# Row kurtosis on one core: more row sums on VectorE from whole-row loads, and wide dummy matmuls in the tail

## Chip, core and metric

The kernel runs on one NeuronCore of a Trainium2 chip. The metric is the device time of one execution in microseconds, given as the median over several runs. Less is better.

## What is computed

The input `x` has 1024 rows of 8192 float32 values. For each row the kernel returns the excess kurtosis:

```python
mean = np.mean(x, axis=-1, keepdims=True)
std = np.std(x, axis=-1, keepdims=True)
z = (x - mean) / (std + 1e-8)
return (np.mean(z ** 4, axis=-1) - 3).astype(np.float32)
```

So every element is read once from HBM (33.55 MB) and is used three times: in the row's sum (for the mean), in the sum of squared deviations, and in the sum of their fourth powers.

## The kernel before

**Groups.** The rows are cut into 18 groups, numbered 0 to 17 (`GROUPS`, L16). An entry is (k, pieces, elements of ACT, engine of the sum). A row is spread over k partitions, so a group has 128/k rows and a tile of 128 x 8192/k. From group 3 on k is 2 and a tile is 128 x 4096 float32, 2.1 MB. `pieces` says into how many DMAs the tile's load is cut and how wide each is. The last entry says which engine adds up the row: 'DVE' (VectorE), 'PE' (TensorE), or 'both' for the last group.

**Loads.** `load(i)` issues the DMAs of group i on SyncE's queue (L134). There are five tile buffers (`SLOT_OF`, L39). `load_next` issues a load only after the group that held the buffer before is through its fourth powers, and in program order.

**Mean (`mean`, L163).** In a 'DVE' group `added_halves` (L157) runs one VectorE instruction, which adds the left half of the tile to the right half and accumulates over the row; it needs the whole tile. A small matmul with a block matrix (L167) then adds up the k partitions of a row. In a 'PE' group `transposed_sums` (L140) runs 32 transposes of 128 x 128 which accumulate into one PSUM tile `tps`; they can start with the first piece. VectorE reduces that tile (`pair_sums`, `red`, L146), and a small matmul (L176) gives the mean. In both cases ScalarE copies the result to `nmu` (L178). In what follows "the mean matmul" is L167 or L176.

**Squares and fourth powers.** `square` (L184) is one ScalarE instruction over the tile, which writes (x - mean)^2 in place and accumulates it. `fourth_act` (L191) squares the first columns again on ScalarE, as many as the group's entry says; `fourth_dve` (L196) does the other columns on VectorE.

**Order.** The order is written out by hand. Iteration i of the main loop (L266) issues: `mean(i)`, `square(i)`, `fourth_dve(i-1)`, the next load, steps of `finish`, `fourth_act(i)`. Each engine runs its own instructions in that order. So VectorE reduces or adds up group i before it does the fourth powers of group i-1, and TensorE starts the transposes of group i+1 behind the mean matmul of group i.

**Finish.** `finish` (L210) turns the sums of a batch of groups into results, in three steps: matmul `p` (L225), reciprocal and `fac` on VectorE; then `sq` on ScalarE, matmul `pf`, `frow` on ScalarE; then matmuls `pk` (L243), `kr` on VectorE and the output DMA (L247). `STEPS` (L260) says in which iterations the three steps of the first three batches are issued.

**Tail.** The last group's squares are done in two halves, and its fourth powers are split between both engines. `keep_busy(n)` (L205) issues n dummy transposes of a tile of zeros, whose result nobody reads: 28 after the first matmul of the last `finish`, 12 after its third (L217 to L223).

Of the kernel before, what the change touches and what calls it, by code (L numbers as in the profile page):

```python
# [7 lines left out]
f32 = mybir.dt.float32  # L8
# [3 lines left out]
P = 128  # L12
# [5 lines left out]
    (8, [1024], 0, 'DVE'),  # L18
    (4, [2048], 0, 'DVE'),
    (2, [4096], 1280, 'DVE'),  # L20
    (2, [4096], 768, 'DVE'),
    (2, [4096], 1536, 'DVE'),
    (2, [2304, 1792], 640, 'PE'),
    (2, [2304, 1792], 640, 'PE'),
    (2, [2304, 1792], 640, 'PE'),
    (2, [2304, 1792], 640, 'PE'),
    (2, [2304, 1792], 512, 'PE'),
    (2, [2304, 1792], 512, 'PE'),
    (2, [2304, 1792], 512, 'PE'),
    (2, [2304, 1792], 512, 'PE'),  # L30
    (2, [1536, 1536, 1024], 512, 'PE'),
    (2, [1536, 1536, 1024], 512, 'PE'),
    (2, [1536, 1536, 1024], 512, 'PE'),
# [9 lines left out]
def kernel(  # L43
# [5 lines left out]
    nc = tc.nc  # L49
# [14 lines left out]
    psfin = ctx.enter_context(tc.tile_pool(name="psfin", bufs=1, space=bass.MemoryType.PSUM))  # L64
    ctx.enter_context(tc.manual_schedule())

    zeros = const.tile([P, 512], f32, name="zeros")
# [21 lines left out]
    ident = const.tile([P, P], f32, name="ident")  # L89
# [108 lines left out]
            op0=AO.mult, op1=AO.add, accum_out=quads[1 + second][:, j:j + 1])  # L198


    idle = psfin.tile([P, P], f32, name="idle")

    def keep_busy(n):
        for _ in range(n):
            nc.tensor.matmul(idle, lhsT=zeros[:, :P], rhs=ident, start=True, stop=True,  # L205
                             is_transpose=True)

    def finish(b):  # L210
        s2, quads = stats[b[0]]
        n = len(b)
        k = KS[b[0]]
        r = P // k
        sel = blk[k].rearrange("p (r k) -> p r k", k=k)[:, :, 0]
        p2 = psfin.tile([P, n], f32, name="p2")
        if b[-1] == L:  # L217
            nc.tensor.matmul(p2[:, :n - 1], lhsT=blk[k], rhs=s2[:, :n - 1], start=True, stop=True)
            keep_busy(28)
            for j in (0, 1):  # L220
                nc.tensor.matmul(p2[:, n - 1:], lhsT=blk[k], rhs=s2[:, n - 1 + j:n + j],  # L221
                                 start=j == 0, stop=j == 1)
            keep_busy(12)  # L223
        else:
            nc.tensor.matmul(p2, lhsT=blk[k], rhs=s2, start=True, stop=True)  # L225
        rec = fin.tile([P, n], f32, name="rec")
        nc.vector.reciprocal(rec, p2)
        fac = fin.tile([P, n], f32, name="fac")
        nc.vector.scalar_tensor_tensor(
            out=fac, in0=rec, scalar=-1.0, in1=rec, op0=AO.mult, op1=AO.mult)  # L230
        yield
        sq = fin.tile([P, n], f32, name="sq")
        nc.scalar.activation(out=sq, in_=p2, func=AF.Square)
        pf = psfin.tile([n, r], f32, name="pf")
        nc.tensor.matmul(pf, lhsT=fac, rhs=sel, start=True, stop=True)  # L235
        frow = fin.tile([n, r], f32, name="frow")
        nc.scalar.activation(out=frow, in_=pf, func=AF.Copy, scale=-float(n_cols) / k)
        yield
        pk = psfin.tile([n, r], f32, name="pk")
        terms = [(q, sel) for q in (quads[1], quads[0])] + [(sq, sel3[k])]  # L240
        terms += [(q, sel) for q in quads[2:]]
        for j, (t, m) in enumerate(terms):
            nc.tensor.matmul(pk, lhsT=t, rhs=m, start=j == 0, stop=j == len(terms) - 1)  # L243
        kr = fin.tile([n, r], f32, name="kr")
        nc.vector.tensor_mul(kr, pk, frow)
        dst = out[ROWS[b[0]]:ROWS[b[-1] + 1]].rearrange("(g r) -> g r", r=r)
        nc.sync.dma_start(out=dst, in_=kr)  # L247
# [5 lines left out]
    def load_next(done):  # L253
        while to_load and held.get(SLOT_OF[to_load[0]], -1) <= done:
            i = to_load.pop(0)
            held[SLOT_OF[i]] = i
            load(i)

    load_next(-1)
    STEPS = [(7, 8, 9), (9, 10, 11), (13, 14, 15)]  # L260
    steps = {}
    for b, ats in zip(BATCHES[:-1], STEPS):
        f = finish(b)
        for at in ats:
            steps.setdefault(at, []).append(f)
# [11 lines left out]
    a = GROUPS[L][2]  # L277
    h = n_cols // KS[L] // 2
    f = finish(BATCHES[-1])
    mean(L)  # L280
    square(L, h, 2 * h)
# [38 lines left out]
```

## Time and profile before

| what | value |
|---|---|
| median of 7 runs | 98.27 us (97.74 to 98.72) |
| the profiled execution: its own time | 97.97 us |
| the profiled execution: span of the core's instructions | 96.3 us |
| PE, DVE, ACT busy | 61.5, 75.7, 79.9 us |
| busy share of the main DMA queue | 84.8% of the span |
| HBM read | 33.55 MB |
| last load lands | 84.7 us after the span's start |

PE is TensorE, DVE is VectorE, ACT is ScalarE, SP is SyncE. Times within the profile are counted from the span's start. Busy shares are means over an opening, a long steady part and a tail. Between the end of the span and the execution's own time lie 1.7 us that no instruction shows.

### The profile page before, as it was taken

What the parts mean: (1) busy time and instruction counts of PE and PEld (TensorE: products, weight loads), DVE (VectorE), ACT (ScalarE), POOL (GpSimd) and SP (SyncE); (2) the same over time, 40 slices, a digit from 0 to 9 for tenths busy, and PEclk for the clock granted to TensorE, in tenths of its full rate; (3) what the DMA queues carried; (4) which work ended last, traced back from release to release, by engine and by line L of the source; (5) the groups of instructions that cost most, each with busy time, mean ns of one, the idle gap of its engine ahead of it and who ended that gap; (6) DMA issues with size and microseconds to landing.
All of it is one profiled execution on the core that took longest, in us unless ns stands there. A gap on an engine that the chain in (4) does not pass through costs nothing.

```text
span 96.3 us, 1389 instructions
## 1 busy us (share of the span) xinstructions
PE 61.5 (64%) x504; PEld 57.2 (59%) x504; DVE 75.7 (79%) x77; ACT 79.9 (83%) x96; POOL 6.1 (6%) x22
## 2 busy tenths in 40 slices
PE   0040201011099797979797979797979797969670
PEld 0040201010099696969696969696969696959560
DVE  2256719899994394989797979699999797999960
ACT  6065350999999699999999999999999998999950
POOL 6980000000000000000000000000000000000000
PEclk9999999999999999999999999999999999999999
DMA  2999999999999999999999999999999999400000
GB/s 89 371 344 429 429 429 436 436 429 409 406 435 365 430 417 439 421 414 422 426 417 425 419 406 430 415 411 408 421 412 416 409 419 401 188 0 7 0 0 4
DMA packets 5083, 33.65 MB, mean 350 GB/s; under 512 B 596, under 2 KB 596, under 8 KB 3540
## 3 DMA queue, kind: packets, MB, share of 16 engines
q1 hardware_dynamic: 5076, 33.56, 84.8%
q8 instruction: 4, 0.07, 0.3%
q14 instruction: 3, 0.02, 0.1%
HBM read 33.55 MB, written 0.00 MB: 349 GB/s over the span
## 4 chain that ended last, share of the span: by engine, by line
PE 42%; ACT 25%; DMA 14%; DVE 13%; issue 3%; DVEq 0%
PE tps L140 32%; ACT xt L184 21%; DMA xt<-in_x_dram 14%; DVE junk L157 5%; DVE xt L196 4%; DVE red L146 4%; PE mps L176 3%; ACT xt L191 2%; PE pk L243 2%; PE idle L205 1%; PE mps L167 1%; ACT nmu L178 1%; PE pf L235 1%; PE p L225 1%; PE p L221 0%
## 5 line engine op out<-in xcount | busy, mean ns | idle before, releaser
L184 ACT ACTIVATE xt<-xt,nmu 128x4096 f32<-128x4096 f32 (+2 forms) x19 | 60.4, 3178 | 0.6
L196 DVE CUSTOM_DVE_ANT_0 xt<-xt 128x3584 f32<-128x3584 f32 (+7 forms) x19 | 59.4, 3130 | 0.9 <-ACT xt L184 0.6
L140 PE MATMUL tps<-ident,xt 128*128 128x128 f32 x380 | 46.5, 282 | 0.0
L140 PEld LDWEIGHTS tps<-ident,xt 128*128 128x128 f32 x380 | 43.9, 147 | 0.9 <-DMA xt<-in_x_dram 0.4
L167 PE MATMUL mps<-part,blk 128*128 128x1 f32 x12 | 3.4, 350 | 23.8 <-DVE part L157 23.8
L167 PEld LDWEIGHTS mps<-part,blk 128*128 128x128 f32 x12 | 3.0, 311 | 24.1 <-ACT xt L184 9.2
L157 DVE CUSTOM_DVE_ANT_0 junk<-xt 128x2048 bf16<-128x2048 f32 (+3 forms) x7 | 10.1, 1448 | 7.1 <-DMA xt<-in_x_dram 7.1
L191 ACT ACTIVATE xt<-xt 128x512 f32<-128x512 f32 (+5 forms) x15 | 12.5, 832 | 0.4
L178 ACT COPY nmu<-mps 128x1 f32<-128x1 f32 x18 | 2.8, 155 | 11.2 <-PE mps L167 9.5
L146 DVE TENSOR_REDUCE red<-tps 128x128 f32<-128x256 f32 x12 | 5.1, 424 | 8.3 <-PE tps L140 8.3
L176 PEld LDWEIGHTS mps<-negcol,red 128*128 128x128 f32 x22 | 3.3, 188 | 8.7 <-DVE red L146 3.0
L176 PE MATMUL mps<-negcol,red 128*128 128x1 f32 x22 | 4.0, 251 | 6.3 <-DVE red L146 4.5
L205 PE MATMUL idle<-ident,zeros 128*128 128x128 f32 x40 | 4.8, 274 | 0.0
L205 PEld LDWEIGHTS idle<-ident,zeros 128*128 128x128 f32 x40 | 4.5, 145 | 0.0
L184 ACT ACTIVATION_READ_ACCUMULATOR xt<-xt,nmu 128x1 f32 x19 | 3.5, 186 | 0.0
L191 ACT ACTIVATION_READ_ACCUMULATOR xt<-xt 128x1 f32 x15 | 2.8, 186 | 0.0
L79 POOL TENSOR_SCALAR_AFFINE_SELECT blk<-blk 128x128 f32<-128x128 f32 x3 | 2.1, 716 | 0.2
L69 ACT ACT_TABLE_LOAD x1 | 1.3, 1283 | 0.8 <-PEq L304 0.8
L243 PE MATMUL pk<-blk,q 128*5 128x64 f32 (+3 forms) x18 | 1.7, 217 | 0.0
L82 POOL TENSOR_SCALAR_AFFINE_SELECT blk<-blk 128x128 f32<-128x128 f32 x3 | 1.6, 542 | 0.2
L196 DVE DVE_READ_ACCUMULATOR2_ANT q<- 128x1 f32 x19 | 1.6, 82 | 0.0
L68 DVE MEMSET zeros<- 128x512 f32 x1 | 0.5, 485 | 1.0 <-PEq L304 1.0
(33 smaller groups left out, 16.4 us busy)
## 6 DMA issues: line engine op xcount, KB each, us to landing
xt<-in_x_dram SPq DMA_DIRECT2D x8, 1152.0 KB, 11.0
xt<-in_x_dram SPq DMA_DIRECT2D x8, 896.0 KB, 12.5
xt<-in_x_dram SPq DMA_DIRECT2D x3, 2048.0 KB, 11.1
xt<-in_x_dram SPq DMA_DIRECT2D x7, 768.0 KB, 11.2
xt<-in_x_dram SPq DMA_DIRECT2D x5, 512.0 KB, 11.3
xt<-in_x_dram SPq DMA_DIRECT2D x1, 1024.0 KB, 7.2
xt<-in_x_dram SPq DMA_DIRECT2D x1, 640.0 KB, 11.6
xt<-in_x_dram SPq DMA_DIRECT2D x1, 384.0 KB, 10.6
```

The source lines that it names most:

```text
L79: nc.gpsimd.affine_select(out=v, in_=v, pattern=[[-k, r], [0, k]], base=0, channel_multiplier=1, compare_op=AO.is_ge, fill=0.0)
L140: nc.tensor.matmul(tps, lhsT=xts[i][:, c:c + P], rhs=ident, start=c == 0, stop=c == w - P, is_transpose=True)
L146: nc.vector.tensor_reduce(out=red.rearrange("p (r k) -> p r k", k=2), in_=tps.rearrange("p (r k) -> p r k", k=2).unsqueeze(2).to_broadcast ...
L157: nc.vector.tensor_tensor_reduce(out=junk[:, :h], in0=t[:, :h], in1=t[:, h:], scale=1.0, scalar=0.0, op0=AO.add, op1=AO.add, accum_out=part)
L167: nc.tensor.matmul(mps, lhsT=blk[k], rhs=added_halves(i, 0), start=True, stop=True)
L176: nc.tensor.matmul(mps, lhsT=pair_sums(tps), rhs=negcol, start=True, stop=True)
L178: nc.scalar.copy(nmu, mps)
L184: nc.scalar.activation(out=t, in_=t, func=AF.Square, bias=nmus[i], accum_out=s2[:, j + second:j + second + 1])
L191: nc.scalar.activation(out=t, in_=t, func=AF.Square, accum_out=quads[0][:, j:j + 1])
L196: nc.vector.tensor_tensor_reduce(out=t, in0=t, in1=t, scale=1.0, scalar=0.0, op0=AO.mult, op1=AO.add, accum_out=quads[1 + second][:, j:j + 1])
L205: nc.tensor.matmul(idle, lhsT=zeros[:, :P], rhs=ident, start=True, stop=True, is_transpose=True)
L243: nc.tensor.matmul(pk, lhsT=t, rhs=m, start=j == 0, stop=j == len(terms) - 1)
```

## The change

Groups 6 and 7 become 'DVE' groups: their tiles are loaded by one DMA each instead of two, and VectorE adds up the rows; groups 8 to 13 stay 'PE' with two pieces. The number of columns whose fourth powers ACT does changes in groups 4 to 13. The finish steps of the first two batches are issued two iterations later. In the tail 28 and 12 dummy transposes of 128 columns become 4 and 1 dummy matmuls of 512 columns, of zeros by zeros.

```diff
     (2, [4096], 1280, 'DVE'),
-    (2, [4096], 768, 'DVE'),
+    (2, [4096], 1024, 'DVE'),
+    (2, [4096], 1152, 'DVE'),
+    (2, [4096], 1280, 'DVE'),
     (2, [4096], 1536, 'DVE'),
-    (2, [2304, 1792], 640, 'PE'),
-    (2, [2304, 1792], 640, 'PE'),
-    (2, [2304, 1792], 640, 'PE'),
-    (2, [2304, 1792], 640, 'PE'),
-    (2, [2304, 1792], 512, 'PE'),
-    (2, [2304, 1792], 512, 'PE'),
-    (2, [2304, 1792], 512, 'PE'),
-    (2, [2304, 1792], 512, 'PE'),
+    (2, [2304, 1792], 576, 'PE'),
+    (2, [2304, 1792], 576, 'PE'),
+    (2, [2304, 1792], 576, 'PE'),
+    (2, [2304, 1792], 576, 'PE'),
+    (2, [2304, 1792], 576, 'PE'),
+    (2, [2304, 1792], 576, 'PE'),
     (2, [1536, 1536, 1024], 512, 'PE'),
...
-    idle = psfin.tile([P, P], f32, name="idle")
+    idle = psfin.tile([P, 512], f32, name="idle")
 
     def keep_busy(n):
         for _ in range(n):
-            nc.tensor.matmul(idle, lhsT=zeros[:, :P], rhs=ident, start=True, stop=True,
-                             is_transpose=True)
+            nc.tensor.matmul(idle, lhsT=zeros[:, :P], rhs=zeros, start=True, stop=True)
...
-            keep_busy(28)
+            keep_busy(4)
...
-            keep_busy(12)
+            keep_busy(1)
...
-    STEPS = [(7, 8, 9), (9, 10, 11), (13, 14, 15)]
+    STEPS = [(9, 10, 11), (11, 12, 13), (13, 14, 15)]
```

## The prediction

> **What bounds the kernel now.** I read the busy slices first. From slice 1 on the DMA row is full until 84 us, and PE starts its long work only in slice 11:
>
> ```profile
> PE   0040201011099797979797979797979797969670
> ...
> DMA  2999999999999999999999999999999999400000
> ```
>
> A full DMA row does not say that anybody waits for it. The view of waits does:
>
> ```profile
> DVE red L146 <- PE tps L140: 8.3, 11, 2.9
> ...
> PEld tps L140 <- DMA xt<-in_x_dram: 0.4, 2, 0.2
> ```
>
> Once the PE groups run, the transposes wait 0.4 us in all for loads, while VectorE's reduction waits for the transposes in 11 groups. So the steady part goes at the pace of a loop through PE and DVE: 32 transposes, reduction, mean matmul, and only then the next 32. PE's timeline shows it, and its start:
>
> ```profile
> 26.60 0.56 PE L167 MATMUL mps<-part,blk 128*128 128x1 f32 x2 [4.67 <-DVE part L157]
> 27.02 5.86 PE L140 MATMUL tps<-ident,xt 128*128 128x128 f32 x32
> 33.48 0.35 PE L176 MATMUL mps<-negcol,red 128*128 128x1 f32 x2 [0.61 <-DVE red L146]
> 33.70 3.69 PE L140 MATMUL tps<-ident,xt 128*128 128x128 f32 x32
> 38.00 0.35 PE L176 MATMUL mps<-negcol,red 128*128 128x1 f32 x2 [0.61 <-ACT xt L184]
> 38.21 0.36 PE L225 MATMUL p<-s,blk 128*128 128x2 f32 x2
> 38.44 3.69 PE L140 MATMUL tps<-ident,xt 128*128 128x128 f32 x32
> 42.73 0.35 PE L176 MATMUL mps<-negcol,red 128*128 128x1 f32 x2 [0.61 <-ACT xt L184]
> ```
>
> A bare lap, from one mean matmul to the next, is 38.00 - 33.48 = 4.52 us. With a finish step in it it is 4.65 to 4.99. The mean matmul of group 16 comes at 81.41, so groups 8 to 16 take 81.41 - 42.73 = 38.68 us. A group's bytes need 5.0 us (the trace's records of the loads' semaphores have the last pieces of groups 10 and 16 at 49.67 and 79.67: 30.0 us for six groups). So the loop gains on the loads by about 0.2 us a lap, and just catches up: in group 13 and in group 17 a piece is late by 0.1 us each. ACT is third in line: it runs back to back, idle before `nmu` for 1.08 us at 33.87 and hardly again. Three queues thus end within half a microsecond of each other, and whatever falls behind by more sets the end.
>
> The first lap matters most. Group 6's 32 transposes take 5.86 us, the next group's 3.69. No load explains it, since group 6 is complete at 28.62. The window view of L140 counts the transposes:
>
> ```profile
> 27.10:31.30 4.20, 4.20 (x20) 4.20 (x21) 1.00 0.98 388
> 34.00:37.20 3.20, 3.20 (x32) 3.15 (x29) 1.00 1.00 420
> ```
>
> 20 in 4.2 us against 32 in 3.2 us (each count has some that overlap an edge); start to start it is 213 ns until 31.5 and 109 ns after. The array starts from rest at half speed and needs 4.5 us of work to rise. (The column after the counts, the granted clock, says 1.00 for both; this trace's record of it begins only with the rise at 31.48, so the spacing is what to read.) The price is 5.86 - 3.69 = 2.17 us, paid once.
>
> **The change, part by part.** *Where PE starts.* Groups 6 and 7 go to DVE, so the start from rest moves to group 8. DVE's order is then: halves of 5, fourths of 4, halves of 6, fourths of 5, halves of 7. Up to 26.37 nothing changes. From start to start a halves-add takes 2.21 us (18.93 to 21.14), the fourths of 2816 columns 3.02 (21.14 to 24.16) and of 3328 columns 3.54 (26.37 to 29.91), so by the straight line 3072 columns take 3.28 and 2944 take 3.15. Fourths of 4 start at 26.37, halves of 6 at 29.65 (the tile landed at 28.62), fourths of 5 at 31.86, halves of 7 at 35.01 (landed 33.93). Before, group 5's halves started at 24.16 and the first transposes at 27.02, 2.86 us later. So group 8's transposes start at 35.01 + 2.86 = 37.87, against 38.44 now: 0.57 us earlier, and group 8's first piece landed at 36.73.
>
> *The start from rest.* Now from first transpose to mean matmul it is 33.48 - 27.02 = 6.46 us cold, 42.73 - 38.44 = 4.29 warm. Group 8's mean matmul comes at 37.87 + 6.46 = 44.33 instead of 42.73: **+1.60 us**. Bounds: 0 extra if PE were already at full speed (as at 33.70), and 32 x (213 - 109) ns = 3.3 if the whole group ran slow. I take 2.17, the one row that shows a start after such sparse work: in both kernels PE has before it only a pair of mean matmuls every 5 us.
>
> The Trainium skill speaks against the move here: TensorE: Matmul & The Clock Gate, Part 1, says that the array idles at half clock, rises after about 3.4 us of sustained work, and that its window runs freely, so the ramp differs from run to run. By its 3.4 us, an estimate, 16 transposes would be slow, 1.7 us instead of 2.17, and the sum below would be 0.5 smaller. Part 4 of the same page says that transposes do not raise the clock; the trace disagrees, for nothing but transposes ran from 27.02 to the rise at 31.48.
>
> *The loop behind it.* Groups 8 to 16 have the same laps. The first `p` step (0.21 us: 42.73 - 38.00 less 4.52) now lies inside this stretch; the lap of group 13 loses its late piece (66.96 - 62.23 = 4.73 without a step, 0.21 over a bare one). They cancel: 38.68 us again. The loop cannot win the 1.60 back, because its own latency is its pace; that the loads land 5.0 us apart no longer matters when it runs behind them.
>
> *ACT.* Fourths on ACT grow from 9728 to 11264 columns in groups 3 to 16, 1536 x (1487 - 627)/1024 ns = 1.29 us. Its idle time of 1.08 at 33.87 disappears, since groups 6 and 7 no longer wait for slow transposes. A lap of ACT, square to square, is 4.67 us at 512 columns and 0.84 ns more a column: 5.10, 5.21, 5.31 and 5.53 for groups 4 to 7, so from 22.49, where group 4's square starts as before, group 8's could start at 43.64, ahead of its mean. Behind that a lap at 576 columns is 4.72, below the loop's 4.83 (38.68/8). Hidden.
>
> *DVE.* Two halves-adds more (4.4 us), two reductions fewer (0.8), 1536 columns fewer (1.6): +2.0 us, laid out above up to 37.2; behind that it idled 0.2 to 0.7 us before each reduction, and the fourths get 64 columns shorter or longer (0.07). Hidden.
>
> *Loads.* A whole-row DMA instead of two: 4.90 us a group (groups 2 to 4 land at 8.96, 13.85, 18.76) against 4.96 (groups 10 to 12), so 0.1 us earlier for two groups; nobody waits. Tile buffers come free up to 1.6 us later from group 7 on, but loads land 10 to 12 us after issue at 5 us a group, so over 5 us of work stand in the queue. The finish steps issue the same instructions as before, two iterations later; their output DMAs stand on SP behind `kr`, which DVE does right after the fourths that the next load waits for anyway. Zero; a buffer that came later than those 5 us would move the end by the excess.
>
> *Tail.* A dummy matmul in float32 is two instructions (`p` and `pk` show two each). Start to start an instruction of 64 columns takes 57 ns in `pk` and one of 128 columns 109 ns, so 512 columns should take about 0.43 us.
>
> ```profile
> 86.65 3.25 PE L205 MATMUL idle<-ident,zeros 128*128 128x128 f32 x28
> ...
> 90.93 0.38 PE L221 MATMUL p<-s,blk 128*128 128x1 f32 x2 [0.91 <-ACT xt L184]
> 91.17 1.51 PE L205 MATMUL idle<-ident,zeros 128*128 128x128 f32 x12
> 92.61 0.28 PE L235 MATMUL pf<-blk,fac 128*5 128x64 f32 x2
> ```
>
> Four take 8 x 0.43 = 3.4 us instead of 3.1, and there are 0.91 us of slack behind them. One takes 0.9 instead of 1.3: `fac` ends at 92.28 and `pf` waits for the dummies until 92.61. `pf` gains 0.3, but the last `pk` needs the fourths that end at 92.86, and started at 93.06; so 0.14 is left: **-0.14 us**. Bounds: 0, and -0.3.
>
> **Sum.** +1.60 - 0.14 = +1.46 us. On the profiled execution 97.97 + 1.46 = 99.43; it lies 0.30 below the median, and with the median it is 99.73. I take 99.6 us. With the ramp's bounds the forecast's own range is 98.8 to 100.8.
>
> **Rivals.** *Faster.* If PE is at speed when group 8 starts, its mean matmul comes at 37.87 + 4.29 = 42.16, the loop is again stopped by the loads alone, and what counts is that loads come 0.1 to 0.3 us earlier and the tail 0.14 to 0.3 shorter: 97.6 to 98.0, here 97.8. It decides when the ramp costs less than 0.57 us. The 213 ns after five sparse mean matmuls speak against it. *No change: a short ramp.* If the ramp costs 0.6 to 1.0, the loop is late by 0 to 0.4, and with the tail's 0.14 the time is 98.1 to 98.6. ACT does not spoil that: +1.29 for its columns, less its idle 1.08 and two later waits of 0.2 each, is -0.2. For it: the runs of before spread over 1 us, so the ramp may well differ between runs. Against it: 2.17 in the trace. *The dummies do not do what they say:* if a wide one took twice my line, four would take 6.9 us instead of 4.3 of room, and the end moves by 2.6 + 1.6 to 102.5. The straight line from 57 to 109 ns speaks against it.
>
> **Chances.** Forecast 0.67, wide dummies dear 0.04, no change 0.14, faster 0.15. A measurement of this kernel can tell about 0.5% (0.5 us) from no change. So slower 0.71, same 0.14, faster 0.15. The range runs from 98.1, within the no-change case, to 100.8: it leaves out the faster case and the dear dummies.
>
> **What would show it.** Right: the first 32 transposes start near 37.9 and take some 5.9 us; group 16's mean matmul is at 83.0 instead of 81.41; no transpose waits for a load; the four dummies end before `p`. Wrong: the first PE group takes about 3.7 us, or laps below 4.5 us, or a last mean matmul still within 0.3 us of 86.0.

## The result, and the profile after

The changed kernel takes 99.12 us (median of 24 runs, 98.08 to 100.09), the kernel before 98.30 (61 runs, 97.69 to 100.03): 0.82 us more. The ratio of the compared runs is 1.0065, 95% interval 1.0044 to 1.0086. That comparison leaves out runs over 1.5% above a kernel's fastest, so the ratio says a little less than the medians of all runs.

So the direction was the forecast one and 99.12 lies in the range of 98.1 to 100.8, but of the 1.3 us by which 99.6 lay over the median, only six tenths came.

The profiled execution took 98.47 us, span 96.7. PE's timeline, the same stretch as was shown of before, with the last group of VectorE sums in its first line:

```profile
37.51 0.56 PE L167 MATMUL mps<-part,blk 128*128 128x1 f32 x2 [4.80 <-DVE part L157]
37.92 5.13 PE L140 MATMUL tps<-ident,xt 128*128 128x128 f32 x32
43.66 0.35 PE L176 MATMUL mps<-negcol,red 128*128 128x1 f32 x2 [0.61 <-DVE red L146]
43.88 3.69 PE L140 MATMUL tps<-ident,xt 128*128 128x128 f32 x32
48.18 0.35 PE L176 MATMUL mps<-negcol,red 128*128 128x1 f32 x2 [0.61 <-ACT xt L184]
...
82.43 0.38 PE L176 MATMUL mps<-negcol,red 128*128 128x1 f32 x2 [0.52 <-DVE red L146]
```

The start from rest has moved to group 8. The window view of L140 shows its two speeds: 14 transposes in 2.85 us, then 18 (some overlap an edge) in 1.70. (The granted clock behind the counts says 1.00 for both; this trace has no record of a clock change, so here too the spacing is what to read.)

```profile
37.95:40.80 2.85, 2.85 (x14) 2.85 (x15) 1.00 0.99 419
41.20:42.90 1.70, 1.70 (x18) 1.62 (x15) 1.00 1.03 436
```

In the view of waits no transpose waits for a load any more; the line of before, 0.4 us in two waits, is gone, and the reduction's is still there:

```profile
DVE red L146 <- PE tps L140: 7.3, 8, 2.7
```

And the tail, with the last VectorE instruction (`kr`) behind it:

```profile
87.67 3.68 PE L205 MATMUL idle<-zeros 128*128 128x512 f32 x8
91.19 0.28 PE L220 MATMUL p<-s,blk 128*128 128x1 f32 x2
91.95 0.38 PE L220 MATMUL p<-s,blk 128*128 128x1 f32 x2 [0.48 <-ACT xt L184]
92.19 1.10 PE L205 MATMUL idle<-zeros 128*128 128x512 f32 x2
93.36 0.28 PE L234 MATMUL pf<-blk,fac 128*5 128x64 f32 x2
...
94.33 0.21 DVE L244 TENSOR_TENSOR kr<-pk,frow 5x64 f32<-5x64 f32 x1 [0.44 <-PE pk L242]
```

The same instruction before, where the span was 96.25 us (after, exactly, 96.74):

```profile
93.45 0.21 DVE L245 TENSOR_TENSOR kr<-pk,frow 5x64 f32<-5x64 f32 x1 [0.58 <-PE pk L243]
```

Step by step against the sum, in us of the profiled executions (the sum has no term for the last row, so its forecast is the value of before):

| step | before | forecast | after |
|---|---|---|---|
| first transposes of group 8 | 38.44 | 37.87 | 37.92 |
| that group's 32 transposes take | 3.69 | 5.86 | 5.13 |
| mean matmul of group 8 | 42.73 | 44.33 | 43.66 |
| mean matmuls, group 8 to 16 | 38.68 | 38.68 | 38.77 |
| mean matmul of group 16 | 81.41 | 83.0 | 82.43 |
| second `p` of the last finish to `kr` | 2.52 | 2.38 | 2.38 |
| end of `kr` | 93.66 | | 94.55 |
| end of `kr` to end of span | 2.59 | 2.59 | 2.20 |

Two rows did not come as worked out: the ramp (the slow start from rest) was shorter in this execution, and the end of the program, behind `kr`, was 0.39 us shorter. The two executions are 0.50 us apart, the medians 0.82, not 1.46. What of this holds for the median, a comparison of two single executions can't say. The experiments had to.

### The profile page after: what moved, and what is told of

It reads as the page before. It is cut to its first block, busy times and chain, and to the rows that moved or that the text cites. A ratio compares the mean times of both kernels' runs of the same rounds, so it can differ in the third digit from the quotient of the medians.

```text
span 96.7 us, 1196 instructions
## 1 busy us (share of the span) xinstructions
PE 53.8 (56%) x410; PEld 47.5 (49%) x410; DVE 77.4 (80%) x79; ACT 81.2 (84%) x96; POOL 6.0 (6%) x22
## 4 chain that ended last, share of the span: by engine, by line
DMA 35%; DVE 26%; ACT 15%; PE 12%; issue 8%; DVEq 0%; SPq 0%
DMA xt<-in_x_dram 35%; DVE xt L196 14%; ACT xt L184 13%; DVE junk L157 10%; PE tps L140 9%; ACT xt L191 2%; PE mps L167 1%; PE pk L242 1%; DVE red L146 1%; PE mps L176 1%; ACT nmu L178 1%; DVE q L196 0%; PE p L224 0%; PE pf L234 0%; DVE kr L244 0%
## 5 line engine op out<-in xcount | busy, mean ns | idle before, releaser
L196 DVE CUSTOM_DVE_ANT_0 xt<-xt 128x3520 f32<-128x3520 f32 (+8 forms) x19 | 57.7, 3043 | 1.2 <-ACT nmu L178 1.0
L140 PE MATMUL tps<-ident,xt 128*128 128x128 f32 x316 | 38.0, 280 | 0.0
L140 PEld LDWEIGHTS tps<-ident,xt 128*128 128x128 f32 x316 | 36.4, 146 | 0.4
L167 PE MATMUL mps<-part,blk 128*128 128x1 f32 x16 | 4.5, 349 | 33.6 <-DVE part L157 33.6
L167 PEld LDWEIGHTS mps<-part,blk 128*128 128x128 f32 x16 | 4.0, 310 | 34.0 <-ACT xt L184 19.0
L157 DVE CUSTOM_DVE_ANT_0 junk<-xt 128x2048 bf16<-128x2048 f32 (+3 forms) x9 | 14.6, 1623 | 6.9 <-DMA xt<-in_x_dram 6.9
L191 ACT ACTIVATE xt<-xt 128x576 f32<-128x576 f32 (+6 forms) x15 | 13.8, 917 | 0.4
L205 PE MATMUL idle<-zeros 128*128 128x512 f32 x10 | 4.8, 609 | 0.0
L205 PEld LDWEIGHTS idle<-zeros 128*128 128x128 f32 x10 | 1.7, 191 | 1.4 <-issue 1.4
L100 POOL TENSOR_SCALAR sel<-blk 128x16 f32<-128x16 f32 (+2 forms) x3 | 1.4, 458 | 0.2
```

What stands on the lines that cost most here:

```text
L140: nc.tensor.matmul(tps, lhsT=xts[i][:, c:c + P], rhs=ident, start=c == 0, stop=c == w - P, is_transpose=True)
L157: nc.vector.tensor_tensor_reduce(out=junk[:, :h], in0=t[:, :h], in1=t[:, h:], scale=1.0, scalar=0.0, op0=AO.add, op1=AO.add, accum_out=part)
L167: nc.tensor.matmul(mps, lhsT=blk[k], rhs=added_halves(i, 0), start=True, stop=True)
L191: nc.scalar.activation(out=t, in_=t, func=AF.Square, accum_out=quads[0][:, j:j + 1])
L196: nc.vector.tensor_tensor_reduce(out=t, in0=t, in1=t, scale=1.0, scalar=0.0, op0=AO.mult, op1=AO.add, accum_out=quads[1 + second][:, j:j + 1])
L205: nc.tensor.matmul(idle, lhsT=zeros[:, :P], rhs=zeros, start=True, stop=True)
```

## The experiments

**The tail alone, on the kernel before.** `keep_busy(4)` and `keep_busy(1)` with wide matmuls, nothing else.

> The kernel before with the tail's part of the change alone: 4 and 1 wide dummy matmuls. Theory: 0.14 us faster (0 to 0.3), 98.0 to 98.3; pf waits for fac and no longer for the dummies. Rival (the dummies matter for the clock in the tail, or cost more than a straight line says): 0.3 us or more in either direction.

Measured: 98.11 us (12 runs) against 98.23; ratio 0.9985, interval 0.9957 to 1.0013. It fits 0.14, and can't be told from nothing. In the profile the eight instructions start 0.43 us apart and `p` to `kr` takes 2.38 us instead of 2.52. This execution shows something else as well, which turned out to matter:

```profile
41.68 0.35 PE L176 MATMUL mps<-negcol,red 128*128 128x1 f32 x2 [0.61 <-ACT xt L184]
...
42.85 3.83 PE L140 MATMUL tps<-ident,xt 128*128 128x128 f32 x32 [0.67 <-DMA xt<-in_x_dram]
47.29 0.35 PE L176 MATMUL mps<-negcol,red 128*128 128x1 f32 x2 [0.61 <-ACT xt L191]
```

Its loop reached group 8 at 41.68, one us earlier than in the execution that I had read, but then the loads stopped it, for 0.67 us in group 9 and again later: groups 8 to 16 took 39.93 us instead of 38.68. Its mean matmul of group 16 came at 81.61, no earlier than the 81.41 of the first.

**The groups alone, with the old tail.**

> The changed kernel with the old tail of 28 and 12 transposes: the groups' part of the change alone. Theory: 0.14 us slower than the changed kernel, 99.1 to 99.5, spread over 2 us as it is there; its group 8 starts from rest at 37.9 with a ramp of another length. Rival as for the tail alone: 0.3 us or more in either direction.

Measured: 99.00 us (11 runs, 97.73 to 99.86), ratio 1.0045, interval 1.0009 to 1.0081. That is a little under the 99.1 to 99.5 expected, and can't be told from the changed kernel's 99.12. The cost is the groups' part.

**No start from rest.** Dummy transposes of zeros behind the mean matmuls ahead of the first PE group:

```diff
+    WARM = {4: 23, 5: 38, 6: 38}        # on the kernel before: {3: 23, 4: 38}
     for i in range(L):
         mean(i)
+        for _ in range(WARM.get(i, 0)):
+            nc.tensor.matmul(idle[:, :P], lhsT=zeros[:, :P], rhs=ident, start=True, stop=True,
+                             is_transpose=True)
```

> The changed kernel, with dummy transposes of zeros behind the mean matmuls of groups 4, 5 and 6 (23, 38 and 38), so that TensorE is at full speed when group 8's transposes start. Theory (the start from rest, moved behind the last slack, is the whole cost, and its length differs from execution to execution): the first 32 transposes take 3.7 us instead of 5.1, the loop then runs into the loads again, and the time falls to 97.6 to 98.1 us with runs within 0.9 us of each other. Rival (VectorE's longer row of work or ScalarE's 1536 columns are the cost): within 0.3 us of the changed kernel, 98.8 to 99.4.

> The kernel before, with 23 and 38 dummy transposes behind the mean matmuls of groups 3 and 4, so that its start from rest, in group 6, is gone too. Theory: it pays the start from rest as well, but most of that is covered by the loads, which set the end when the loop is early: the gain is only 0.2 to 0.6 us (97.7 to 98.1), and runs lie within 0.9 us. Rival (the loop alone sets the end of both kernels): the whole 2 us are gained, 96.3.

Measured: the changed kernel at speed takes 98.02 us (12 runs, 96.97 to 98.41), ratio to before 0.996, interval 0.993 to 0.999: 1.1 us are gained, and it beats both kernels. The kernel before at speed takes 98.21 (97.80 to 98.63), ratio 0.9993, interval 0.9965 to 1.002: nothing is gained, less than I had expected. So the start from rest is the cost in the one, and costs nothing that can be told in the other. The runs of the changed kernel at speed spread over 1.44 us, more than the 0.9 expected. PE's timeline of the changed kernel at speed, then of the kernel before at speed:

```profile
38.04 3.77 PE L140 MATMUL tps<-ident,xt 128*128 128x128 f32 x32 [0.20 <-DMA xt<-in_x_dram]
42.42 0.35 PE L176 MATMUL mps<-negcol,red 128*128 128x1 f32 x2 [0.61 <-DVE red L146]
```

```profile
26.84 3.69 PE L140 MATMUL tps<-ident,xt 128*128 128x128 f32 x32
31.14 0.35 PE L176 MATMUL mps<-negcol,red 128*128 128x1 f32 x2 [0.61 <-DVE red L146]
33.07 3.94 PE L140 MATMUL tps<-ident,xt 128*128 128x128 f32 x32 [1.58 <-DMA xt<-in_x_dram]
```

The second is 2.3 us ahead at group 6 (31.14 against 33.48), and gives 1.58 of them straight to the loads. Its group 16 comes at 81.86.

**Fewer loads.** To see the loop without the loads, the last 512 of 4096 columns of groups 7 and 9 to 16 were not loaded (old values stay; the squares take the data times 0.01), in four kernels: before, before at speed, changed, changed at speed.

```diff
         for w in pieces:
-            nc.sync.dma_start(out=xt[:, c:c + w], in_=src[:, c:c + w])
+            m = w - 512 * (i in CUT and c + w == n_cols // k)
+            nc.sync.dma_start(out=xt[:, c:c + m], in_=src[:, c:c + m])
```

> The kernel before with 512 of 4096 columns left out of the loads of groups 7 and 9 to 16 (old values stay there, and the squares take the data times 0.01 so that nothing overflows): 2.4 MB less to load, so loads run up to 5 us ahead. Theory (before, loads and the loop end together, and a stall of the loads moves the end): the loop alone is left as a bound, start from rest included; 97.6 to 98.1 us, 0.2 to 0.6 faster, and as widely spread as the changed kernel (2 us). Rival (loads never matter): 98.3.

> The same shortened loads, and TensorE kept at speed ahead of group 6 as in the second experiment. Theory (in the kernel before the start from rest costs nothing because the loads cover it; without that cover its absence is worth its full length until ScalarE binds): 96.5 to 97.0 us, 1.3 to 1.8 below the kernel before. Rival (the start from rest never cost the kernel before anything, for another reason than the loads): as without the dummies.

> The changed kernel with the same shortened loads. Theory (its loop runs behind the loads, so they do not matter any more): within 0.3 us of the changed kernel, 98.8 to 99.3, spread 2 us. Rival (loads still set its end): 0.5 us or more faster.

> The changed kernel kept at speed and with the shortened loads of the earlier experiment: neither ramp nor loads can bind. Theory: its mean matmul of group 8 comes at 42.2 instead of 44.4, the loop or ScalarE's own row of work is the bound, 97.2 to 97.7 us, that is 1.6 to 2.1 below the changed kernel with shortened loads (99.27) and 0.3 to 0.8 below the changed kernel kept at speed with whole loads (98.02); spread under 1.2 us. Rival (something other than ramp and loads holds the changed kernel at 98): 97.9 or more.

Medians of all runs, us:

| | whole loads | shortened loads |
|---|---|---|
| before | 98.30 | 97.44 (96.44 to 98.40, 12 runs) |
| before, at speed | 98.21 | 98.07 (96.42 to 98.50, 6 runs) |
| changed | 99.12 | 99.27 (98.78 to 99.78, 6 runs) |
| changed, at speed | 98.02 | 97.62 (96.61 to 97.86, 12 runs) |

The kernel before gains 0.86 from shorter loads (ratio 0.9892, interval 0.9844 to 0.9939), more than the 0.2 to 0.6 expected, and its runs then spread over 2 us like those of the changed kernel. The changed kernel gains nothing. In the profiles of before and changed with shortened loads no transpose waits for a load. So the loads hold the one and not the other. A fall of TensorE's clock, as described next, is not that hold: of the 17 runs of the kernel before that were taken beside the 97.44, one has it, and the other 16 have a median of 98.32. With the loads out of the way the two kernels differ by 99.27 - 97.44 = 1.83 us: the later loop, less what the tail and the end of the program gain. At speed the changed kernel gets 1.65 us back, the late start from rest, and its 97.62 lies in the expected 97.2 to 97.7. These are medians of 6 to 12 runs that spread over 1 to 2 us, good to a few tenths.

The kernel before at speed with shortened loads missed its 96.5 to 97.0 in four of six runs. Two took 96.42 and 96.47; the other four took 97.75 to 98.50, and all four have a mean granted clock of 0.982, against 0.995 and 0.997. The profiled execution is one of the four. Its PE timeline, and the window view with the engines' busy times, granted clock, DMA share and GB/s:

```profile
31.00 0.35 PE L179 MATMUL mps<-negcol,red 128*128 128x1 f32 x2 [0.61 <-DVE red L149]
32.70 5.38 PE L143 MATMUL tps<-ident,xt 128*128 128x128 f32 x32 [1.35 <-DMA xt<-in_x_dram]
```

```profile
27.00:30.30 3.30, 3.30 (x32) 3.15 (x29) 2.88 (x2) 3.27 (x4) 0.00 (x0) 1.00 1.03 404
33.02:36.40 3.38, 3.38 (x19) 3.38 (x17) 0.90 (x2) 3.38 (x2) 0.00 (x0) 0.50 1.01 425
```

PE came so early that it stood idle for 1.35 us before group 7, whose load had not landed. The clock fell to 0.50 at 33.02, for 3.41 us, and those 32 transposes took 5.38 us. A loop ahead of its loads can pay for it twice. The two undisturbed runs bear the theory out, the other four show a cost that it had left out.

**All but the groups, at speed.** The kernel before with the warm-up and the wide dummies.

> The kernel before, with TensorE kept at speed ahead of group 6 and with the wide dummies in the tail: all of the change but the groups' part, and no start from rest. Theory (with the ramp gone both versions run into the same loads): 0.1 to 0.2 us below the kernel before, 98.0 to 98.2, the same as the changed kernel kept at speed (98.02). Rival (the groups' part gains something of its own once the ramp is gone): 0.3 us or more above 98.02.

Measured: 98.11 us (12 runs, 97.65 to 98.68), ratio 0.9979, interval 0.9951 to 1.0007. That is within 0.1 us of the changed kernel at speed. Without the start from rest the groups' part costs nothing and gains nothing that can be told. But the two are equal only at the end of the span: in the profiles `kr` ends at 93.83 here and at 94.30 in the changed kernel at speed, whose end behind it is 0.39 us shorter (2.20 against 2.59). So some 0.3 us of VectorE's sums, ScalarE's columns or the loads may show before `kr`; two executions can't tell that from chance. Six of the twelve runs here have a granted clock of 0.982, and they are no slower than the others (98.14 against 98.05).

**How long a start from rest is.** Bursts of 56 transposes and pauses, nothing else.

> No kurtosis at all: 20 bursts of 56 transposes, with pauses between them that VectorE's work sets, each of another length (6 to 9 us), so that the start from rest is seen 20 times in one execution. Theory (the rise comes at the end of a window that runs freely, so its distance from the burst's start differs): the slow part of a burst lasts between 3 and 6 us, spread evenly, not always the 4.5 us that the kernel before showed; the price against full speed, half of it, 1.4 to 3 us, mean about 2. Rival (a fixed number of slow transposes): 20 or 21 slow transposes in every burst.

Measured, by the starts of the transposes in the trace: 13 to 28 of them stand 213 ns apart, the rise 2.83 to 6.03 us after the burst's start. The price is 104 ns (213 - 109) each: 1.4 to 2.9 us, and 2.2 on the mean (about 21 of them). Three of the twenty bursts in PE's timeline, and the granted clock in the page's slices:

```profile
24.17 7.78 PE L86 MATMUL tps<-ident,xt 128*128 128x128 f32 x56 [6.53 <-DVE xt L95]
...
55.24 9.28 PE L86 MATMUL tps<-ident,xt 128*128 128x128 f32 x56 [7.41 <-DVE xt L95]
...
205.26 7.69 PE L86 MATMUL tps<-ident,xt 128*128 128x128 f32 x56 [7.34 <-DVE xt L95]
```

```profile
PEclk9968585858585858585867678785858585858585
```

All of its clock changes lie a whole number of 3.413 us apart: a grid of its own, which the program does not set. A stretch of this grid with 2.66 us of transposes in it (the burst at 55.24) did not end with a rise; one with 2.83 (the burst at 205.26) did. This agrees with the free-running window of 3.4 us of the Trainium skill (TensorE: Matmul & The Clock Gate, Part 1).

**Two pieces again for groups 6 and 7, and fewer DMAs in the kernel before.** The span ended 0.39 us sooner after `kr` in the changed kernel, which no step had foretold. The first kernel takes [2304, 1792] for groups 6 and 7, still 'DVE'; the second [4096] for groups 8 and 9, still 'PE'.

> The changed kernel with groups 6 and 7 loaded in two pieces again (2304 and 1792 columns); their sums stay on VectorE. In all profiles so far the span ends 2.6 us after the last VectorE instruction with the old groups and 2.2 us after it with the new ones, with the warm-up and the tail of either kind. Theory A (whole-row loads mean two DMAs and their waits fewer on SyncE's queue, and its end of program is 0.4 us shorter for that): 2.6 us here, and the median 0.3 to 0.5 above the changed kernel. Theory B (the 0.4 us belong to something else): 2.2 us, and the time within 0.2 us of the changed kernel, since its loop runs behind the loads.

> The kernel before with groups 8 and 9 loaded by one DMA each, sums still on TensorE: two DMAs fewer on SyncE's queue. Theory A: the span ends 2.2 us after the last VectorE instruction. Theory B: 2.6 us. The transposes of groups 8 and 9 can start only with the whole tile, so the loop may lose up to 1 us there; the time itself tells nothing.

Measured: 99.14 us with split loads (12 runs, 97.59 to 100.11), the changed kernel's 99.12, and its span ends 2.07 us after `kr`. So whole-row loads as such gain nothing, and the number of DMAs does not set the 0.39 us. The second kernel's span ends 2.50 us after `kr`. In the kernel before a pause of 0.43 us stands between two of SyncE's last instructions, and in the changed kernel there is none; in the second kernel here it stands later, between two others. The later finish steps and ScalarE's columns were not varied by themselves, so what sets it stays open. The second kernel's one execution took 100.38 us. Its group 9 waited for the whole tile, and again the clock fell, at 44.65:

```profile
44.22 5.35 PE L140 MATMUL tps<-ident,xt 128*128 128x128 f32 x32 [1.30 <-DMA xt<-in_x_dram]
```

## Why the prediction was right in its mechanism and wrong in its size

**Right: what is paid.** The start from rest moved from group 6 to group 8, and what it cost came back when it was taken away: 1.10 us with whole loads (99.12 to 98.02), 1.65 without their hold (99.27 to 97.62). The first transposes of group 8 were forecast at 37.87 and came at 37.92.

**Right: nobody wins it back in the changed kernel.** Groups 8 to 16 took 38.77 us against 38.68, and 2.4 MB fewer loads changed nothing (99.27).

**Right, as far as can be told: the covers.** ACT's 1536 columns, DVE's sums, the whole-row loads and the later finish steps cost nothing at the end of the span (98.02 against 98.11 at speed, 99.14 against 99.12 split); up to 0.3 us before `kr` could stand behind the shorter end. The tail's -0.14 is the measured difference of the profiles.

**Wrong: the end of the program.** The sum is +1.60 for the loop and -0.14 for the tail. It puts what follows `kr` at nothing and gives no reason. That stretch became 0.39 us shorter, and not by chance: it is 2.19 to 2.21 us in the five profiles with the changed groups and whole-row loads, with the warm-up or without, with either tail, with either length of loads, and 2.58 to 2.59 in the six with the old groups. With this term the sum is +1.07 instead of +1.46, and it is the largest part of what was missing to the measured 0.82. Why the end is shorter stays open.

**Wrong: what the kernel before pays already.** The second step that failed is the base of the sum. "The loop behind it" gave the loads 0.21 us of the kernel before, from the one late piece in group 13, and the sum then took the 0.30 us between that execution and the median as common to both kernels. (The late pieces in groups 13 and 17 are 0.2 us each in the view of waits, not 0.1.) Both sizes come from an execution in which the loads hardly stood in the way. The median one loses 0.86 us to the loads (98.30 against 97.44 when they are shortened), and the changed kernel's loop, late anyway, loses none. So the +1.60 comes near the net of two sizes that the prediction did not have. Without the loads' hold the loop alone is later by 1.83 us and by what the tail and the end of the program take off, 1.83 + 0.14 + 0.39 = 2.36, and 0.86 of that only take the place of a wait for loads. What is left is 1.50 (1.35 with the changed kernel's 99.12 in place of 99.27), near 1.60 in part by luck. A late loop and late loads don't add up; the later of them counts.

What is left between 1.07 and 0.82 can't be told from the scatter of the medians. Its sign is that of the ramp. Forecast was 2.17; the twenty bursts give 2.2 on the mean, and the eight profiles of kernels that have it 14 to 24 slow transposes, about 18.5 on the mean, 1.9 us. A shorter ramp helps the changed kernel and hardly the kernel before, which gains nothing even without one (98.21). The ramp's price differs by up to 1.5 us from one execution to the next, so the one price from one profile could not be trusted to better than that. In the four profiled executions with the changed groups and the whole start from rest, more slow transposes go roughly with more time: 14, 17, 19 and 24, and 98.47, 98.75, 99.41 (with shortened loads) and 99.37 us. This is probably also what spreads the changed kernel's runs over 2 us; at speed they lie within 1.4.

The rival "no change: a short ramp" named the right quantity and asked too little of it. An estimate: the changed kernel is 0.82 us over the kernel before with a ramp of 1.9 us, and a shorter ramp saves its difference as long as the loads do not bind, so one of about 1.1 us would have been free.

## What to carry to other kernels

Where two chains end within a few tenths of a microsecond of each other, a single profile shows only the one that was later in that execution; a step added to one chain costs its length less what the median execution, not the profiled one, already waits for the other. Take each chain's own time first, by cutting the other short. A step of which the sum says nothing, here the end of the program, is a term too, and can be read in the profiles of both kernels. If an engine needs a start from rest, let it warm up on dummy work while it has nothing to do: here 99 dummy transposes, put where TensorE was idle, turned a loss of 0.65% into a gain of 0.4% (ratios 1.0065 and 0.996).

## What was not expected of the hardware

- Idle gaps of 1.30 and 1.35 us in the loop went with a fall of TensorE's clock to half for a whole 3.41 us, in the two kernels above; after a gap of 1.58 us in the kernel before at speed it stayed up (32 transposes in 3.94 us). The gap alone does not decide it. On the grid of 3.41 us on which the clock changes, the stretch that ended with the fall was idle for 1.96 and 1.91 us, since the 0.61 us for which TensorE waits before the mean matmul lay in it too. The gap of 1.58 us lay across an edge of the grid, and its two stretches were idle for 1.14 and 1.06 us; the most without a fall, ahead of the tail, was 1.40 (the kernel before at speed with the wide dummies). The Trainium skill (TensorE: Matmul & The Clock Gate, section Why this matters for your kernels) warns of gaps over about 3 us between bursts; here shorter ones sufficed.
- The loads lose some tenths of a microsecond between 24 and 34 us in some executions and not in others, with all of them queued: 383 GB/s from 28 to 32 us in the kernel before, 446 in the changed groups with the old tail. These lines are the window view, busy times of PE, PEld, DVE, ACT and POOL, granted clock, DMA share and GB/s, first of the former, then of the latter. Why was not found.

```profile
28.00:32.00 4.00, 4.00 (x23) 4.00 (x22) 2.00 (x2) 3.97 (x3) 0.00 (x0) 1.00 0.96 383
```

```profile
28.00:32.00 4.00, 0.27 (x2) 0.30 (x2) 4.00 (x5) 3.97 (x3) 0.00 (x0) 1.00 1.04 446
```
